# A transformer trunk whose feed-forward weights are summed on the fly: the third weight sum as a loaded block minus the first, on VectorE

## The chip, the cores and the metric

The kernel runs on one core of a Trainium2 chip. The metric is the device time of one execution in microseconds (us), lower is better. A core has TensorE (PE, matrix products; its weight loads are shown apart as PEld), VectorE (DVE), ScalarE (ACT), GpSimd (POOL) and SyncE (SP). Each of them works through its own list of instructions strictly in the order that was written. Loads from memory are issued by SP, ACT or POOL and carried out by 16 DMA engines that all share. In this kernel POOL issues only transfers that add what they carry to what stands at the target; plain loads are issued by SP.

## The reference

The reference is a small encoder trunk: 512 tokens and 16 learned meta tokens, width 1024, two layers. Each layer is

```python
h = h + 0.5 * swiglu(rmsnorm(h, gains[l, 0]), w_gate[l, 0], w_up[l, 0], w_down[l, 0])
h = h + mixer(rmsnorm(h, gains[l, 1]), ...)      # gated linear attention and softmax attention, merged
h = h + 0.5 * swiglu(rmsnorm(h, gains[l, 2]), w_gate[l, 1], w_up[l, 1], w_down[l, 1])
```

with `swiglu(x) = (silu(x @ w_gate) * (x @ w_up)) @ w_down`, gate and up 1024 x 2816, down 2816 x 1024, all in float32. A last norm follows, and the meta tokens are dropped. So there are four feed-forward parts (FFNs), named (layer, which) below: (0, 0), (0, 1), (1, 0), (1, 1). The change touches only them.

## The kernel before, in words

Every float32 matrix is split into a high and a low part in a rounded format that TensorE takes at a faster rate; a product is three matmuls (high x high, high x low, low x high). For each loaded or summed block of weights of 128 x 1024 values this means a copy on ScalarE that makes the high part (line 264) and a subtraction on VectorE that makes the low part (line 265). The pair is called the split.

The FFNs save matmuls with a scheme of seven block products where eight would be usual. The weights of an operation are four blocks, named 11, 12, 21 and 22, and the seven products, numbered 1 to 7, use these operands:

- products 1, 2 and 4: blocks 11, 12 and 22 as they are loaded (`DIRECT`);
- product 5: the first sum, 21 + 22 (`s1`);
- product 7: the third sum, 21 - 11 (`s3`);
- product 6: the second sum, 22 + 21 - 11 (`s2`);
- product 3: the fourth sum, 22 + 21 - 11 - 12 (`s4`).

An FFN has 15 such operations, numbered i. Numbers 0 to 10 are pairs of 128-column tiles of gate and up, in three groups of 4, 4 and 3 pairs. After each of the first two groups come two down quads (numbers 11 and 12, then 13 and 14), that is the part of the down product that belongs to the group; the third group's part is done in the usual way. Each product of an operation is 24 matmuls (lines 571 and 685). The order of all products is written out in `ffn_steps`: in a group, product 1 of the next pair comes ahead of product 7 of the current one, and so on, and in the change from a group to its quads the products of the last pair, the two quads and the next pair are interleaved.

The accumulators that TensorE fills are emptied by ScalarE (line 575, `snapshot`) and VectorE (lines 581 to 615). In the change to the quads VectorE and ScalarE also make the quads' operands from the pairs' results (lines 625, 646, 647, 651) and VectorE adds the quads' products to h (line 693).

`Weights` brings the blocks. `use(j)` first makes (splits) the loads up to a few ahead of product j and then fetches (issues the loads) up to nine ahead. Blocks go to a pool of three buffers (`raw`); `s3` and `s4` share three buffers (tag `wsa`, the long pool), `s1` and `s2` another three (tag `wsb`, the short pool). The sums are made so:

- `s3`: ScalarE writes the negated block 11 (`negative`, line 203), then POOL issues a transfer that adds block 21 from memory (`add`, line 208). This happens when block 11 is fetched (for the first two pairs of the first FFN, `OPENING`, when it is made).
- `s2`: SP loads block 22, then POOL issues a transfer that adds `s3` to it, from buffer to buffer.
- `s1`: SP loads block 21, then POOL issues a transfer that adds block 22 from memory.
- `s4`: for the first two pairs a negation of block 12 and a transfer that adds `s2`; from the third pair on VectorE subtracts block 12 from `s2` (line 233), when product 6 is made.

The order of each engine's instructions is not the order of the program. A planner simulates the kernel with its own estimates of durations and landings, and whenever an engine is free in that simulation it gives it the ready instruction that comes first in the program. So an instruction whose inputs the planner holds to be there may be placed ahead of others that stand earlier in the program and are not yet ready; on the chip the order is then fixed, and an engine waits at each instruction until its inputs have come. `W.behind` and `issue_after` keep the copies of line 264 behind certain instructions of ScalarE.

Of the kernel before, what the change touches and what calls it, by code (L numbers as in the profile page):

```python
# [14 lines left out]
ALU = mybir.AluOpType  # L15
# [31 lines left out]
OPENING = ((0, 0), 0), ((0, 0), 1)  # L47
# [101 lines left out]
NPAIR = FF // P // 2  # L149
# [21 lines left out]
class Weights:  # L171
# [34 lines left out]
    def add(self, t, src):  # L206

        self.nc.gpsimd.dma_start(t, src, accum_op=ALU.add)  # L208

    def sums(self, f, i, product, w):  # L210


        got = self.summed
        if product == "1":
            s3 = self.negative(f, i, "s3", w)
            self.add(s3, self.dram(f, i, "21"))
            s2 = self.block(f, i, "22", self.short, "wsb")
            self.add(s2, s3)
            got[f, i, "7"], got[f, i, "6"] = s3, s2
        if product == "12"[(f, i) in OPENING]:  # L220
            s1 = self.block(f, i, "21", self.short, "wsb")
            self.add(s1, self.dram(f, i, "22"))
            got[f, i, "5"] = s1
        late = 2 <= i
        if product == "2" and not late:
            s4 = self.negative(f, i, "s4", w)
            self.add(s4, got[f, i, "6"])
            got[f, i, "3"] = s4
        if product == "2" and late:
            self.kept = w  # L230
        if product == "6" and late:
            s4 = self.long.tile([P, SLAB], F32, tag="wsa", name=f"s4_{f[0]}{f[1]}_{i}")
            self.nc.vector.tensor_tensor(s4, w, self.kept, ALU.subtract)
            got[f, i, "3"] = s4

    def fetch(self, upto):

        while self.fetched < min(upto, len(self.loads)):
            load = self.loads[self.fetched]
            if isinstance(load, int):  # L240
                w = self.raw.tile([P, SLAB], F32, tag="raw", name=f"raw{load}")
                self.nc.sync.dma_start(w, self.wts[load])
                self.raws[self.fetched] = w
            elif load[2] in DIRECT:
                self.raws[self.fetched] = self.block(*load[:2], DIRECT[load[2]])
                if load[2] == "1" and load[:2] not in OPENING:
                    self.sums(*load, self.raws[self.fetched])
            self.fetched += 1

    def make(self, upto):  # L250
        nc = self.nc
        while self.made < min(upto, len(self.loads)):
            self.fetch(self.made + 1)
            s = self.made
            load = self.loads[s]
            w = self.raws.pop(s, None)
            if w is None:
                w = self.summed.pop(load)
            hi = self.hi_pool.tile([P, SLAB], F32R, tag="whi", name=f"whi{s}")
            lo = self.lo_pool.tile([P, SLAB], F32R, tag="wlo", name=f"wlo{s}")  # L260
            for a in np.split(np.arange(SLAB), 2 if s == 0 else 1):
                cs = slice(a[0], a[-1] + 1)
                with self.tc.issue_after(self.behind) if self.behind else nullcontext():
                    nc.scalar.copy(hi[:, cs], w[:, cs])  # L264
                nc.vector.tensor_tensor(lo[:, cs], w[:, cs], hi[:, cs].bitcast(F32), ALU.subtract)  # L265
            self.got[s] = (hi, lo)
            self.got.pop(s - 12, None)
            self.made += 1
            if not isinstance(load, int) and (load[2] in "26" or load[2] == "1" and load[:2] in OPENING):
                self.sums(*load, w)  # L270

    def use(self, j, ahead=AHEAD_MADE):
# [29 lines left out]
def build(tc, ctx, xt, wts, win, par, w2, const, umask, out):  # L302
# [243 lines left out]
    def ffn(l, f, norm, done, following):  # L546

        x, rs, up, n = norm.x, None, None, live[0]
        w = n // 2
        pools = open_pools("left", psum=("s2",), c=4, s2=2)  # L550
        made, hid, sums, raw, sets = {}, {}, {}, {}, {}
        risen = iter(range(KC))

# [636 lines left out]
    def finish_chunk(c):  # L1190
        fin.square(c)
        gain(c, slice(0, SEQ))

    def ending(sums, operand, rs):

        table("abs_reciprocal_sqrt_and_small")
# [146 lines left out]
```

## Time and profile before

| | before |
|---|---|
| median of 3 runs | 2238.69 us (2238.67 to 2239.18) |
| the profiled execution | 2233.24 us |
| its span, first to last instruction | 2231.4 us |
| granted TensorE clock, mean | 0.996 |
| TensorE busy | 2170.3 us, 97% |
| VectorE busy | 1700.7 us, 76% |
| ScalarE busy | 1244.2 us, 56% |
| POOL busy | 164.4 us, 7% |
| moved by DMA | 330.29 MB, 148 GB/s |

The page of the profile lists each engine's busy time, the costliest groups of instructions (line, engine, operation, output <- inputs, shape, count | busy us, mean ns of one | idle time ahead of them and what ended it), and the DMA issues with the median time from issue to landing. The list of waits says who waited for whom: us in total, times, longest. A row of the timeline is start, duration, engine, line, operation, and in brackets the idle time ahead of it and who ended it. A row of a table of stretches is the stretch, its length, then for TensorE, its weight loads, VectorE, ScalarE and POOL the busy us and the number of instructions, and last the granted clock, the share of the DMA engines and GB/s. In the names, `whi` and `wlo` are the high and low part of a block, `s` is a buffer of `s3` or `s4`, `w` any other block, `ss` an accumulator, `c` and `g` buffers of results and operands. The four FFNs lie at about 0 to 340, 750 to 1090, 1100 to 1450 and 1840 to 2200 us.

### The profile page before, as it was taken

What the parts mean: (1) busy time and instruction counts of PE and PEld (TensorE: products, weight loads), DVE (VectorE), ACT (ScalarE), POOL (GpSimd) and SP (SyncE); (2) the same over time, 40 slices, a digit from 0 to 9 for tenths busy, and PEclk for the clock granted to TensorE, in tenths of its full rate; (3) what the DMA queues carried; (4) which work ended last, traced back from release to release, by engine and by line L of the source; (5) the groups of instructions that cost most, each with busy time, mean ns of one, the idle gap of its engine ahead of it and who ended that gap; (6) DMA issues with size and microseconds to landing.
All of it is one profiled execution on the core that took longest, in us unless ns stands there. A gap on an engine that the chain in (4) does not pass through costs nothing. (4 is left out here: it accounts for less than half of the span.)

```text
span 2231.4 us, 40120 instructions
## 1 busy us (share of the span) xinstructions
PE 2170.3 (97%) x16506; PEld 2075.3 (93%) x16506; DVE 1700.7 (76%) x2623; ACT 1244.2 (56%) x1815; POOL 164.4 (7%) x192
## 2 busy tenths in 40 slices
PE   7999999999999999999999999999999999999898
PEld 7999999989999999999999999999788888999897
DVE  8877877577876679687788778676779768687777
ACT  8555555345784555454675455553557836545553
POOL 1111100000000011111011111000000001111100
PEclk9999999999999999999999999999999999999999
DMA  9877753212114577777668777421111237677761
GB/s 280 226 190 203 198 150 109 77 48 72 43 39 133 133 189 191 211 203 190 179 166 212 190 208 202 139 100 67 57 67 57 88 104 199 177 200 191 187 180 67
DMA packets 92647, 330.29 MB, mean 148 GB/s; under 512 B 10288, under 2 KB 12720, under 8 KB 92464
## 3 DMA queue, kind: packets, MB, share of 16 engines
q1 hardware_dynamic: 63440, 226.65, 28.2%
q0 software_dynamic: 27072, 98.58, 24.4%
q8 instruction: 130, 2.13, 0.4%
q10 hardware_dynamic: 1952, 2.50, 0.4%
q14 instruction: 53, 0.43, 0.1%
HBM read 289.94 MB, written 2.10 MB: 131 GB/s over the span
## 5 line engine op out<-in xcount | busy, mean ns | idle before, releaser
L571 PE MATMUL ss<-xc,whi 128*128 128x264 f32 (+1 forms) x4928 | 909.2, 286 | 26.1 <-ACT c L575 16.5
L571 PEld LDWEIGHTS ss<-xc,whi 128*128 128x128 f32 x4928 | 768.8, 190 | 31.1 <-ACT c L575 18.8
L571 PE MATMUL ss<-xc,wlo 128*128 128x264 f32 (+1 forms) x2464 | 702.8, 285 | 2.7 <-DVE wlo L265 2.7
L265 DVE TENSOR_TENSOR wlo<-w,whi 128x1024 fp32r<-128x1024 f32 (+1 forms) x301 | 365.3, 1216 | 152.8 <-ACT whi L264 152.7
L571 PEld LDWEIGHTS ss<-xc,wlo 128*128 128x128 f32 x2464 | 467.4, 190 | 4.3 <-DVE wlo L265 4.3
L264 ACT CAST whi<-w 128x1024 fp32r<-128x1024 f32 (+1 forms) x301 | 312.1, 1048 | 136.2 <-PE ss L571 52.2
L438 PE MATMUL mm<-x,whi 128*128 128x264 f32 (+1 forms) x1712 | 384.8, 315 | 0.0
L438 PEld LDWEIGHTS mm<-x,whi 128*128 128x128 f32 x1712 | 278.4, 188 | 16.6 <-issue 1.0
L438 PE MATMUL mm<-x,wlo 128*128 128x264 f32 (+1 forms) x856 | 266.1, 315 | 0.0
L685 PE MATMUL ss<-g,whi 128*128 128x264 f32 (+1 forms) x1280 | 239.5, 285 | 4.4 <-DVE h L693 3.1
L264 ACT CAST whi<-raw 128x1024 fp32r<-128x1024 f32 x126 | 132.0, 1048 | 163.6 <-PE mm L438 102.8
L685 PEld LDWEIGHTS ss<-g,whi 128*128 128x128 f32 x1280 | 198.6, 188 | 7.0 <-ACT whi L264 3.4
L265 DVE TENSOR_TENSOR wlo<-raw,whi 128x1024 fp32r<-128x1024 f32 x126 | 153.9, 1221 | 59.3 <-ACT whi L264 58.4
L685 PE MATMUL ss<-g,wlo 128*128 128x264 f32 (+1 forms) x640 | 181.2, 283 | 0.0
L575 ACT COPY c<-ss 128x528 f32<-128x528 f32 (+1 forms) x132 | 78.3, 593 | 181.6 <-PE ss L571 181.4
L265 DVE TENSOR_TENSOR wlo<-s,whi 128x1024 fp32r<-128x1024 f32 x120 | 146.5, 1221 | 37.5 <-ACT whi L264 37.5
L438 PEld LDWEIGHTS mm<-x,wlo 128*128 128x128 f32 x856 | 159.6, 188 | 8.5 <-issue 0.7
L438 PE MATMUL ss<-g,whi 128*128 128x264 f32 (+2 forms) x900 | 166.2, 299 | 0.0
L438 PEld LDWEIGHTS ss<-g,whi 128*128 128x128 f32 x900 | 131.7, 188 | 5.3
L264 ACT CAST whi<-s 128x1024 fp32r<-128x1024 f32 x120 | 126.1, 1051 | 10.9 <-PE ss L571 7.2
L208 POOL DMA_DIRECT2D w<-win x60 | 54.5, 908 | 1029.3 <-DVE wlo L265 410.3
L203 ACT ACTIVATE s<-w 128x1024 f32<-128x1024 f32 x68 | 71.6, 1056 | 89.7 <-DMA w<-win 77.9
(265 smaller groups left out, 3405.4 us busy)
## 6 DMA issues: line engine op xcount, KB each, us to landing
w<-win SPq DMA_DIRECT2D x299, 512.0 KB, 5.4
raw<-wts SPq DMA_DIRECT2D x126, 512.0 KB, 3.2
s<-win POOLq DMA_DIRECT2D x60, 512.0 KB, 5.2
w<-s POOLq DMA_DIRECT2D x60, 512.0 KB, 5.5
w<-win POOLq DMA_DIRECT2D x60, 512.0 KB, 7.5
s<-w POOLq DMA_DIRECT2D x8, 512.0 KB, 8.4
h<-xt SPq DMA_DIRECT2D x3, 528.0 KB, 6.3
out<-h ACTq DMA_DIRECT2D x4, 256.0 KB, 2.4
```

The lines of the kernel that those rows point to most:

```text
L203: self.nc.scalar.activation(t, w, AF.Copy, scale=-1.0)
L208: self.nc.gpsimd.dma_start(t, src, accum_op=ALU.add)
L264: nc.scalar.copy(hi[:, cs], w[:, cs])
L265: nc.vector.tensor_tensor(lo[:, cs], w[:, cs], hi[:, cs].bitcast(F32), ALU.subtract)
L438: TE.matmul(acc.half[i][:width], lhs, rhs[:, acc.spans[i]], start=first, stop=last)
L571: TE.matmul(acc[:, j], a[:, j, k], b[:, at], start=bool(begin and k == 0 and i == 0), stop=k == len(x) - 1 and i == 2, skip_group_check=no ...
L575: W.behind = S.copy(part(st, q), acc).ins
L685: TE.matmul(acc[:, j], a[:, j, k], xs[b][:, k], start=bool(begin and k == 0 and i == 0), stop=k == 3 and i == 2, skip_group_check=not begin)
```

## The change

For pairs from the third on and for all down quads (`2 <= i`) there is no negation any more. When block 11 is fetched, SP loads block 21 into the buffer of `s3` with a plain transfer, and block 22 into the buffer of `s2`. When product 1 has been made (block 11 has been split), VectorE subtracts block 11 from `s3` in place. The second sum then differs: for pairs (gate and up, `i < NPAIR`) VectorE adds `s3` to `s2` in place when product 2 has been made; for the quads POOL still issues the transfer that adds `s3` to `s2`, now after VectorE's subtraction. The first and the fourth sum are made as before, and the first two pairs of each FFN too.

```diff
+    def begin_sums(self, f, i, w=None):
         got = self.summed
-        if product == "1":
+        s3 = None
+        if i < 2:
             s3 = self.negative(f, i, "s3", w)
             self.add(s3, self.dram(f, i, "21"))
-            s2 = self.block(f, i, "22", self.short, "wsb")
+        else:
+            s3 = self.block(f, i, "21", self.long, "wsa")
+        s2 = self.block(f, i, "22", self.short, "wsb")
+        if i < 2:
             self.add(s2, s3)
+        got[f, i, "7"], got[f, i, "6"] = s3, s2
+        if (f, i) not in OPENING:
+            self.first_sum(f, i)
...
+        if (f, i) in OPENING and product in "12":
+            (self.begin_sums if product == "1" else self.first_sum)(f, i, *[w] * (product == "1"))
+        if i < 2:
+            if product == "2":
+                s4 = self.negative(f, i, "s4", w)
+                self.add(s4, got[f, i, "6"])
+                got[f, i, "3"] = s4
+        elif product == "1":
+            V.tensor_tensor(got[f, i, "7"], got[f, i, "7"], w, ALU.subtract)
+            if not i < NPAIR:
+                self.add(got[f, i, "6"], got[f, i, "7"])
+        elif product == "2":
             self.kept = w
-        if product == "6" and late:
+            if i < NPAIR:
+                V.tensor_tensor(got[f, i, "6"], got[f, i, "6"], got[f, i, "7"], ALU.add)
+        elif product == "6":
             s4 = self.long.tile([P, SLAB], F32, tag="wsa", name=f"s4_{f[0]}{f[1]}_{i}")
-            self.nc.vector.tensor_tensor(s4, w, self.kept, ALU.subtract)
+            V.tensor_tensor(s4, w, self.kept, ALU.subtract)
             got[f, i, "3"] = s4
...
                 if load[2] == "1" and load[:2] not in OPENING:
-                    self.sums(*load, self.raws[self.fetched])
+                    self.begin_sums(*load[:2], self.raws[self.fetched])
...
-            if not isinstance(load, int) and (load[2] in "26" or load[2] == "1" and load[:2] in OPENING):
+            if not isinstance(load, int) and load[2] in "126":
                 self.sums(*load, w)
```

`first_sum` holds the two lines that made `s1` before.

More of the change, by code (lines that the diff above doesn't have):

```diff
@@ L208, in add @@
         self.nc.gpsimd.dma_start(t, src, accum_op=ALU.add)
-    def sums(self, f, i, product, w):
+    def begin_sums(self, f, i, w=None):
         got = self.summed
-        if product == "1":
+        s3 = None
+        if i < 2:
             s3 = self.negative(f, i, "s3", w)
             self.add(s3, self.dram(f, i, "21"))
-            s2 = self.block(f, i, "22", self.short, "wsb")
+        else:
+            s3 = self.block(f, i, "21", self.long, "wsa")
+        s2 = self.block(f, i, "22", self.short, "wsb")
+        if i < 2:
@@ L218, in sums @@
             self.add(s2, s3)
[L219 to L229, printed above, removed]
+        got[f, i, "7"], got[f, i, "6"] = s3, s2
@@ new lines, in begin_sums, with first_sum, sums @@
+        if (f, i) not in OPENING:
+            self.first_sum(f, i)
+    def first_sum(self, f, i):
+        s1 = self.block(f, i, "21", self.short, "wsb")
+        self.add(s1, self.dram(f, i, "22"))
+        self.summed[f, i, "5"] = s1
+    def sums(self, f, i, product, w):
+        got, V = self.summed, self.nc.vector
+        if (f, i) in OPENING and product in "12":
[10 more added lines that the diff above has]
+        elif product == "2":
```

## The prediction

> **What bounds the kernel now.** I read the page's first part and its groups, then the waits, then the idle stretches of TensorE row by row, then what ScalarE and VectorE did ahead of the longest, and last the stretches in which VectorE is full. From the page, the list of waits and the groups by line:
>
> ```profile
> PE 2170.3 (97%) x16506; PEld 2075.3 (93%) x16506; DVE 1700.7 (76%) x2623; ACT 1244.2 (56%) x1815; POOL 164.4 (7%) x192
> L203 ACT ACTIVATE s<-w 128x1024 f32<-128x1024 f32 x68 | 71.6, 1056 | 89.7 <-DMA w<-win 77.9
> ACT s L203 <- DMA w<-win: 77.9, 18, 6.3
> PE ss L571 <- ACT c L575: 16.5, 11, 4.8
> L233 DVE TENSOR_TENSOR s<-w,w 128x1024 f32<-128x1024 f32 x52 | 63.4, 1219 | 0.1
> ```
>
> TensorE is busy for 97% of the span, so a change of helper work can win only what TensorE idles (2231.4 - 2170.3 = 61 us, its start and end among it) and what it loses to a lower clock. The second and third lines are the negations that the change removes: ScalarE stood 77.9 us at them, waiting for the block to land, 18 times and up to 6.3 us. Most of those stops cost nothing. The fourth line says where one may: TensorE waited 16.5 us for the copies at line 575 that empty its accumulators. These are its idle rows in the last FFN (first eight), and in an FFN before it at the same steps (last three):
>
> ```profile
> 1945.29 0.38 PE L571 MATMUL ss<-xc,whi 128*128 128x256 f32 x1 [4.84 <-ACT c L575]
> 1964.01 0.35 PE L685 MATMUL ss<-g,whi 128*128 128x256 f32 x1 [1.57 <-DVE h L693]
> 1964.72 0.38 PE L685 MATMUL ss<-c,whi 128*128 128x256 f32 x1 [0.24 <-ACT c L646]
> 1965.98 0.39 PE L685 MATMUL ss<-c,whi 128*128 128x256 f32 x1 [0.88 <-DVE c L647]
> 2076.43 0.58 PE L571 MATMUL ss<-xc,whi 128*128 128x256 f32 x1 [4.79 <-ACT c L575]
> 2095.91 0.35 PE L685 MATMUL ss<-g,whi 128*128 128x256 f32 x1 [1.51 <-DVE h L693]
> 2096.73 0.39 PE L685 MATMUL ss<-c,whi 128*128 128x256 f32 x1 [0.34 <-ACT c L646]
> 2097.99 0.39 PE L685 MATMUL ss<-c,whi 128*128 128x256 f32 x1 [0.88 <-DVE c L647]
> 854.58 0.39 PE L571 MATMUL ss<-xc,whi 128*128 128x264 f32 x1 [0.50 <-ACT c L575]
> 869.51 0.39 PE L685 MATMUL ss<-c,whi 128*128 128x264 f32 x1 [0.37 <-DVE c L647]
> 874.89 0.39 PE L685 MATMUL ss<-c,whi 128*128 128x264 f32 x1 [0.90 <-DVE c L647]
> ```
>
> Both long stops lie in the change from a group of pairs to its down quads. ScalarE in order of time shows why:
>
> ```profile
> 1935.81 0.83 ACT L646 CAST g<-g 128x768 fp32r<-128x768 f32 x1
> 1942.97 1.06 ACT L203 ACTIVATE s<-w 128x1024 f32<-128x1024 f32 x1 [6.33 <-DMA w<-win]
> 1943.93 0.81 ACT L646 CAST c<-g 128x768 fp32r<-128x768 f32 x1
> 1944.66 0.58 ACT L575 COPY c<-ss 128x512 f32<-128x512 f32 x1
> 2074.11 1.06 ACT L203 ACTIVATE s<-w 128x1024 f32<-128x1024 f32 x1 [6.27 <-DMA w<-win]
> ```
>
> The negation for the second quad, whose sum is due only ten products after the block itself, stood 6.33 us at the head of ScalarE; the cast of the operand and the copy that frees TensorE's accumulator were behind it. In the other three FFNs the planner put that copy ahead of the negation, and the same step costs 0.50 us. TensorE's clock fell after both stops:
>
> ```profile
> 1945.00:1950.00 5.00, 4.71 (x27) 4.72 (x28) 3.99 (x6) 2.25 (x4) 0.31 (x1) 0.66 0.58 107
> 1966.00:1970.00 4.00, 4.00 (x21) 4.00 (x22) 3.93 (x4) 0.00 (x0) 0.00 (x0) 0.57 0.02 4
> 2076.00:2083.00 7.00, 6.57 (x33) 6.58 (x34) 4.65 (x7) 3.48 (x5) 1.31 (x2) 0.55 0.52 95
> ```
>
> The number ahead of the last two is the granted clock. Time lost there is (1 - clock) x length.
>
> **The change, part by part.** Pairs 2 to 10 and the four quads are 13 third sums per FFN, 52 in all; 36 of them belong to pairs.
>
> Removed on ScalarE: 52 of the 68 negations, 52 x 1.056 = 54.9 us of an engine that is 56% busy. Their worth is the work that waited behind them.
> (1) The two long stops fall to the 0.50 of the other FFNs: (4.84 - 0.50) + (4.79 - 0.50) = 8.63 us.
> (2) What follows each: 1.57 + 0.24 + 0.88 = 2.69, and 1.51 + 0.34 + 0.88 = 2.73, against 0.37 + 0.90 = 1.27 elsewhere: 1.42 + 1.46 = 2.88 us.
> (3) The clock: 5 x 0.34 + 4 x 0.43 + 7 x 0.45 = 1.70 + 1.72 + 3.15 = 6.57 us.
> (4) Pair 2's negation also stood ahead of such a copy, waiting for a buffer, in two FFNs:
>
> ```profile
> 796.37 1.06 ACT L203 ACTIVATE s<-w 128x1024 f32<-128x1024 f32 x1 [2.52 <-DVE wlo L265]
> 797.96 0.39 PE L571 MATMUL ss<-xc,whi 128*128 128x264 f32 x1 [1.50 <-ACT c L575]
> 1884.18 0.39 PE L571 MATMUL ss<-xc,whi 128*128 128x256 f32 x1 [1.59 <-ACT c L575]
> ```
>
> (1.50 - 0.50) + (1.59 - 0.50) = 2.09 us. All other negations I cost at nothing gained: TensorE showed no idle row behind them.
>
> On (3) the Trainium skill has a rule: "TensorE: Matmul & The Clock Gate", the section on how the gate's oscillation bites, has the array fall to half rate once TensorE idled for a window of about 3.4 us. The first and third drop agree (4.84 and 4.79 us idle); the second does not, since the idle ahead of it was 1.57, 0.24 and 0.88 us. By that rule alone (3) would be 4.85 us and the forecast 1.7 us later.
>
> Added on VectorE: 36 x 2 + 16 = 88 additions and subtractions of 128x1024. Line 233 has the same form at 1219 ns, so 107.3 us of busy time (76% becomes 81%). In a row of full work one costs the pitch to the next, 1.14 us (856.99 to 858.13, below). Between group changes it is covered:
>
> ```profile
> 900.00:950.00 50.00, 50.00 (x412) 50.00 (x412) 33.12 (x39) 24.37 (x29) 6.65 (x8) 1.00 0.79 202
> 1150.00:1200.00 50.00, 49.27 (x404) 49.26 (x404) 42.76 (x58) 29.70 (x37) 6.09 (x7) 1.00 0.75 194
> 862.00:893.00 31.00, 29.65 (x235) 28.71 (x234) 30.52 (x37) 16.79 (x19) 3.49 (x4) 1.00 0.72 191
> ```
>
> At 412 matmuls in 50 us, a pair (7 products of 24) takes 20.4 us, in which VectorE (third number) is busy 33.12/50 x 20.4 = 13.5 us; 2 x 1.14 more leave 4.6 us idle. The second row is the fullest start of an FFN: 42.76 of 50, and some 2.5 pairs x 2.28 = 5.7 us more still fit. In the third, a group change, it is busy 30.52 of 31 us and has no cover. What I count there is two instructions ahead of the 0.90 us row: the second quad's subtraction, and the first quad's fourth sum, which today slips in early because its inputs are there, and which will wait for a later addition by POOL. Against that stands the idle time that today's negation makes on VectorE:
>
> ```profile
> 856.99 1.22 DVE L233 TENSOR_TENSOR s<-w,w 128x1024 f32<-128x1024 f32 x1
> 858.13 0.42 DVE L615 SCALAR_TENSOR_TENSOR c<-ss,rs 128x264 f32<-128x264 f32 x1
> 859.86 1.23 DVE L265 TENSOR_TENSOR wlo<-w,whi 128x1024 fp32r<-128x1024 f32 x1 [1.31 <-ACT whi L264]
> 861.36 0.43 DVE L625 TENSOR_TENSOR g<-c,ss 128x264 f32<-128x264 f32 x1 [0.27 <-ACT c L417]
> 857.83 1.06 ACT L203 ACTIVATE s<-w 128x1024 f32<-128x1024 f32 x1 [2.36 <-DMA w<-win]
> ```
>
> (5) 2 x 1.14 - (1.31 + 0.27) = 0.70 us per change, eight changes: 5.6 us lost. Bounds: nothing, if the planner finds other holes; 3 x 1.14 x 8 = 27.4 us if it finds none and the next pair's subtraction presses too. I take the value nearest to the rows of one change.
>
> Moved: block 21 comes by a plain transfer on SP in place of POOL's accumulating one (52), and 36 accumulating ones from buffer to buffer vanish.
>
> ```profile
> w<-win SPq DMA_DIRECT2D x299, 512.0 KB, 5.4
> s<-win POOLq DMA_DIRECT2D x60, 512.0 KB, 5.2
> w<-s POOLq DMA_DIRECT2D x60, 512.0 KB, 5.5
> SPq L198 <- DVE wlo L265: 666.0, 145, 15.7
> ```
>
> SP gets 52 issues more, each behind a buffer of the long pool that until now the negation waited for. Later in that queue stand the second and the third plain block of the pair; but SP stands up to 15.7 us at such frees already, for the load of block 21 that follows, and every load is issued eight loads ahead of its use, so I cost the issue at 0, and at the most at what a late buffer cost TensorE before, the 2.09 us of (4). POOL loses 88 issues, and what queues behind them (the sum 21 + 22) comes earlier: 0, since no row shows a cast waiting for it. The new wait on VectorE is for block 21's landing: it lands one transfer after block 11, and the subtraction's turn is behind block 11's own split, about six products after the issue: 0, and at the most the second rival's price. If the planner pulls it early into a hole, everything on VectorE queues behind it; that is the second rival.
>
> Sum: -8.63 - 2.88 - 6.57 - 2.09 + 5.6 = -14.6 us. The profiled execution took 2233.24 us, so 2218.6; the median of the runs, 2238.69, stands 5.45 above that execution, and with the same offset the forecast is 2224 us.
>
> **The rivals.** *VectorE becomes the bound in the group changes.* For it speaks the row 862 to 893; against it the holes that vanish with the negations. The gains of 20.2 us are used up at 20.2 / 8 = 2.5 us per change, that is 2.2 uncovered instructions. At the upper bound: 2238.69 - 20.2 + 27.4 = 2245.9. The Trainium skill ("Perfetto Trace Analysis", on the most-contended engine) would judge such a stretch by VectorE's occupancy, 98% there, and so put all added work on the path; the trace before disagrees in part, since TensorE still had 29.65 of 31 us.
>
> *The same trap on VectorE: slower.* The planner believes block 21 landed, pulls a subtraction into a hole, and VectorE stands there as ScalarE did. One such stop is worth half of (1) to (3), 18.08 / 2 = 9.0 us. For it: that is how the negations stood 18 times. Against it: line 233, which is also pulled early, waited 0.1 us in 52 times. Three in place of today's two give 2224.1 + 27.1 = 2251; it decides from two on.
>
> *The stop stays.* The planner writes a new order, and some other instruction (a split whose block is late) takes the place ahead of the copies; only (4) and (5) are seen: 2238.69 - 2.09 + 5.6 = 2242. For it: the plain blocks still take 5.4 us to land; against it: a split's turn is some six products later than the negation's.
>
> **How the numbers follow.** The forecast gets 0.64, faster in all its range. VectorE as the bound gets 0.16, about evenly a small gain, no difference and a loss (0.05, 0.05, 0.06); the trap 0.12, slower; the stop that stays 0.08, no difference that a measurement of this kernel can tell (0.2%, 4.5 us). So faster 0.69, same 0.13, slower 0.18. The likeliest one's own range is 2213 (nothing lost in (5), and 5 us of the shorter waits for line 575 gone too, of their 16.5) to 2233 (little over a third of the gain). The whole range goes up to the first rival's end, 2246, and leaves out the trap with three stops.
>
> **What would show it.** After: no row at line 203 beyond the first two pairs; no idle row of 4 us at line 571 in the last FFN, and a granted clock of 1.00 there; ScalarE near 1189 us, VectorE near 1808; the 0.90 us rows of the group changes grown to some 1.6. It is wrong if VectorE shows stops of several us for a landing, or if the 862 to 893 stretch shows TensorE idle for 3 us more than now.

## The result and the profile after

The changed kernel took 2265.93 us (median; 2258.84 to 2267.80) beside 2238.93 for the kernel before on the same chip: ratio 1.0112, 95% interval 1.0088 to 1.0135. It is slower by 1.1%, 25 us, where 2224 us was forecast, and it lies above the range. Below, a ratio is turned into us by (ratio - 1) x 2239.

The profiled execution took 2266.88 us, span 2265.0. Line 243 is the new subtraction, 249 the new addition; other lines have moved (571 to 590, 575 to 594, 591 to 610, 264 and 265 to 283 and 284, 685 to 704, 693 to 712, 233 to 252). From the page of after, its first part and the groups:

```profile
PE 2187.3 (97%) x16506; PEld 2088.2 (92%) x16506; DVE 1798.7 (79%) x2711; ACT 1195.4 (53%) x1763; POOL 87.6 (4%) x104
...
L243 DVE TENSOR_TENSOR w<-w,w 128x1024 f32<-128x1024 f32 x52 | 63.6, 1222 | 59.6 <-DMA w<-win 53.2 <-issue 6.4
```

From its list of waits (us in total, times, longest):

```profile
DVE w L243 <- DMA w<-win: 53.2, 24, 6.3
...
PE ss L590 <- DVE wlo L284: 14.4, 16, 4.5
...
PE ss L590 <- DVE c L610: 8.1, 7, 1.9
...
PE ss L704 <- DVE h L712: 8.1, 7, 1.5
...
PE ss L590 <- ACT c L594: 6.3, 11, 0.7
```

The stops that the change was to remove are gone: line 594, which answers to line 575 before, cost TensorE 16.5 us with a longest of 4.8, and costs 6.3 with a longest of 0.7. In their place VectorE stands at its new subtraction, 24 times and up to 6.3 us, waiting for block 21 to land. Before, it stood nowhere for such a landing. The rows of VectorE that show it, at the start of the first FFN (first two), in a group change (the next four) and in the last FFN's first group change (last):

```profile
50.05 1.23 DVE L243 TENSOR_TENSOR w<-w,w 128x1024 f32<-128x1024 f32 x1 [2.96 <-DMA w<-win]
...
66.55 1.22 DVE L243 TENSOR_TENSOR w<-w,w 128x1024 f32<-128x1024 f32 x1 [6.34 <-DMA w<-win]
...
877.81 1.23 DVE L243 TENSOR_TENSOR w<-w,w 128x1024 f32<-128x1024 f32 x1 [2.66 <-DMA w<-win]
878.96 0.98 DVE L666 TENSOR_TENSOR c<-g,c 128x792 fp32r<-128x792 f32 x1
879.85 0.70 DVE L610 TENSOR_TENSOR c<-c,ss 128x528 f32<-128x528 f32 x1
...
886.99 1.22 DVE L284 TENSOR_TENSOR wlo<-w,whi 128x1024 fp32r<-128x1024 f32 x1
...
1979.60 1.22 DVE L243 TENSOR_TENSOR w<-w,w 128x1024 f32<-128x1024 f32 x1 [3.52 <-DMA w<-win]
```

By the order of the loads, the row at 886.99 is the split of the block that the subtraction at 877.81 uses: the subtraction runs 9 us ahead of it.

And TensorE at those places, and in the last FFN at the first of the two old stops:

```profile
53.08 0.39 PE L590 MATMUL ss<-xc,wlo 128*128 128x264 f32 x1 [2.68 <-DVE wlo L284]
69.65 0.59 PE L590 MATMUL ss<-xc,wlo 128*128 128x264 f32 x1 [4.46 <-DVE wlo L284]
...
880.70 0.48 PE L590 MATMUL ss<-xc,whi 128*128 128x264 f32 x2 [0.91 <-DVE c L610]
881.74 0.39 PE L590 MATMUL ss<-xc,wlo 128*128 128x264 f32 x1 [0.56 <-DVE wlo L284]
...
1977.48 0.50 PE L590 MATMUL ss<-xc,whi 128*128 128x256 f32 x2 [0.70 <-ACT c L594]
1982.44 0.47 PE L590 MATMUL ss<-xc,whi 128*128 128x256 f32 x2 [1.86 <-DVE c L610]
1983.48 0.39 PE L590 MATMUL ss<-xc,wlo 128*128 128x256 f32 x1 [0.57 <-DVE wlo L284]
```

Behind the stop at 877.81 waits the sum at line 610 that empties an accumulator; TensorE idles 0.91 us for it, and 0.56 for the split behind that. At 1977.48 the old stop of 4.84 us is now 0.70, but 5 us later, behind the stop of 3.52 us at 1979.60, TensorE idles 1.86 + 0.57 us for VectorE. Last, stretches of the clock (the number ahead of the last two):

```profile
69.00:76.00 7.00, 6.35 (x30) 6.35 (x31) 7.00 (x9) 1.04 (x1) 0.00 (x0) 0.52 0.00 0
...
894.90:898.30 3.40, 1.17 (x6) 0.57 (x4) 3.40 (x5) 3.40 (x4) 0.00 (x0) 1.00 0.61 176
898.30:901.70 3.40, 3.38 (x15) 3.38 (x16) 3.40 (x4) 0.53 (x2) 0.00 (x0) 0.51 0.02 5
...
1975.00:1990.00 15.00, 11.87 (x84) 11.28 (x83) 11.30 (x15) 6.35 (x8) 0.87 (x1) 0.89 0.62 174
```

The two profiled executions differ by 2265.0 - 2231.4 = 33.6 us of span. TensorE's idle time grew by (2265.0 - 2187.3) - (2231.4 - 2170.3) = 16.6 us, and the same 16506 matmuls took 2187.3 - 2170.3 = 17.0 us more, at a mean granted clock of 0.990 against 0.996, which by itself gives 2170.3 x (0.996 / 0.990 - 1) = 13 us. So about half the loss is idle time, and most of the other half a slower clock. The profiled execution of before is 5.45 us faster than its median, so this gap is wider than the 25 us.

### The profile page after: what moved, and what is told of

The parts are those of the page before. It is cut to its first block, busy times and chain, and to the rows that moved or that the text cites. A ratio compares the mean times of both kernels' runs of the same rounds, so it can differ in the third digit from the quotient of the medians.

```text
span 2265.0 us, 40086 instructions
## 1 busy us (share of the span) xinstructions
PE 2187.3 (97%) x16506; PEld 2088.2 (92%) x16506; DVE 1798.7 (79%) x2711; ACT 1195.4 (53%) x1763; POOL 87.6 (4%) x104
## 5 line engine op out<-in xcount | busy, mean ns | idle before, releaser
L590 PE MATMUL ss<-xc,whi 128*128 128x264 f32 (+1 forms) x4928 | 913.6, 287 | 24.7 <-ACT whi L283 8.4
L284 DVE TENSOR_TENSOR wlo<-w,whi 128x1024 fp32r<-128x1024 f32 (+1 forms) x353 | 427.0, 1217 | 76.6 <-ACT whi L283 76.2
L283 ACT CAST whi<-w 128x1024 fp32r<-128x1024 f32 (+1 forms) x353 | 366.4, 1048 | 180.1 <-PE ss L590 77.2
L457 PEld LDWEIGHTS mm<-x,whi 128*128 128x128 f32 x1712 | 279.2, 189 | 16.5 <-issue 1.0
L436 ACT ACTIVATE c<-c 128x528 f32<-128x528 f32 (+1 forms) x88 | 56.5, 642 | 132.5 <-DVE c L634 132.2
L704 PEld LDWEIGHTS ss<-g,wlo 128*128 128x128 f32 x640 | 121.9, 190 | 2.5 <-DVE wlo L284 2.5
L704 PE MATMUL ss<-c,whi 128*128 128x264 f32 (+1 forms) x512 | 104.1, 296 | 7.1 <-ACT c L665 5.3
```

What stands on the lines that cost most here:

```text
L436: prev_act[0] = S.activation(*args, **kw).ins
L457: TE.matmul(acc.half[i][:width], lhs, rhs[:, acc.spans[i]], start=first, stop=last)
L590: TE.matmul(acc[:, j], a[:, j, k], b[:, at], start=bool(begin and k == 0 and i == 0), stop=k == len(x) - 1 and i == 2, skip_group_check=no ...
L704: TE.matmul(acc[:, j], a[:, j, k], xs[b][:, k], start=bool(begin and k == 0 and i == 0), stop=k == 3 and i == 2, skip_group_check=not begin)
```

## The experiments

The theory after the result: the planner puts the new subtractions ahead of their landing, and the stops cause the loss. The rival: the added VectorE work itself costs that much, wherever it stands. They are told apart by moving the work without removing it, and by adding the work without the change.

**Place: all new work behind the splits.** Each subtraction and addition may be issued only behind the low part of the split of the block that it uses.

```diff
-                nc.vector.tensor_tensor(lo[:, cs], w[:, cs], hi[:, cs].bitcast(F32), ALU.subtract)
+                self.split_end = nc.vector.tensor_tensor(lo[:, cs], ..., ALU.subtract).ins
...
-            V.tensor_tensor(got[f, i, "7"], got[f, i, "7"], w, ALU.subtract)
+            with self.tc.issue_after(self.split_end):
+                V.tensor_tensor(got[f, i, "7"], got[f, i, "7"], w, ALU.subtract)
```

> The changed kernel, with each new subtraction and addition of VectorE put behind the split of the block after which it stands in the program, so that the planner can't pull it ahead into a hole; the work is the same. If the loss is VectorE standing at subtractions whose block hasn't landed (theory of the stop), the waits of 53.2 us at line 243 vanish, and with them the two long stops at the start of the first FFN (9.9 us) and the 3 us stops in the eight group changes: about 2224 us, as the sum of the prediction had it. If the loss is the 88 added instructions on a full VectorE (theory of the work), the order doesn't help: 2255 us or more.

2240.31 us, ratio 1.0002 [0.9992, 1.0011]: no different from before, and 25 us better than the change as it was. From the waits of this kernel:

```profile
PE ss L706 <- ACT c L667: 11.6, 8, 2.4
DVE s L254 <- DMA w<-w: 10.2, 8, 2.5
```

No wait for a landing is left at the subtraction. A smaller stop takes its place: the quads' fourth sum (line 254) now reads a second sum that POOL's transfer is still adding to. The place of the instructions, not their number, makes the difference between the changed kernel and this one; but the expected gain is still missing.

**Place: one group at a time.** Only the quads' subtractions behind their splits, and only the pairs' subtractions and additions.

```diff
+            with self.tc.issue_after(self.split_end) if not i < NPAIR else nullcontext():   # only the quads
...
+            with self.tc.issue_after(self.split_end) if i < NPAIR else nullcontext():       # only the pairs
```

> As the first, but only the subtractions of the down quads are put behind the split; those of the pairs may still be pulled ahead. Theory of the stop: the group changes are freed, the start of the first FFN keeps its 9.9 us: 2234 us. Theory of the work: 2255 us or more. If the pairs' stops elsewhere cost much too, it stays above 2245.

> The changed kernel with only the pairs' subtractions and additions behind their splits; the quads' subtractions stay where the planner puts them. With all behind it took 2240.3, with only the quads' 2246.5, as it is 2265.9. If the stops add up: 2265.9 - (2246.5 - 2240.3) = 2259.7, and it shows the eight stops of 2.4 to 3.5 us at the second quad's subtraction but not the two at the first FFN's start. If the pairs' early places cause the quads' stops, near 2246.

Only the quads: 2246.53 us, ratio 1.0031 [1.0018, 1.0043]. Only the pairs: 2257.07 us, 1.0073 [1.0058, 1.0089]. The waits at the subtraction, first of the kernel with the quads behind, then of the one with the pairs behind:

```profile
DVE w L244 <- DMA w<-win: 29.0, 14, 6.8
```

```profile
DVE w L244 <- DMA w<-win: 24.7, 8, 4.0
...
PE ss L592 <- DVE c L612: 8.8, 6, 2.2
```

The stops of the change are of two kinds: those of the pairs (14 in the first kernel, 16 of the 24 in the changed one), worth 6.9 - 0.4 = 6.5 us, and eight of the quads, worth 16.3 - 0.4 = 15.9 us. With the 0.4 us of all behind, that is 22.8 of 25.1 us, well inside the intervals. The quads' stops are shorter (24.7 us in all) but cost more than twice as much: they lie in the group changes.

**Work alone, a first try.** The kernel before, with an instruction on `s3` and `s2` where the change has one (a maximum of a buffer with itself, which leaves the values as they are).

```diff
+            if not isinstance(load, int) and load[1] >= 2 and (load[2] == "1" or load[2] == "2" and load[1] < NPAIR):
+                t = self.summed[load[0], load[1], "7" if load[2] == "1" else "6"]
+                with self.tc.issue_after(self.split_end):
+                    nc.vector.tensor_tensor(t, t, t, ALU.max)
```

> The kernel before, with negations and accumulating transfers as they were, and 88 instructions of 128x1024 more on VectorE, each the maximum of a third or second sum with itself, which changes nothing, behind the same splits as in the first run and on data that has long landed. Theory of the work: most of the loss, 2255 to 2266 us. Theory of the stop: the sum's own term for the added work, 5.6 us without the holes that the negations made (1.58 us per group change), so 5.6 to 18 us: 2244 to 2257, and the stops of 4.8 us in the last FFN stay.

2322.17 us, ratio 1.0376 [1.0351, 1.0402]. This misses as a price of work, as its waits show:

```profile
DVE s L274 <- DMA w<-s: 105.7, 29, 11.1
```

The maximum had to wait for POOL's transfer that still read `s3`. It tells something else: 105.7 us of stops on VectorE, with the work, cost 84 us of the kernel's time.

**Work alone, clean.** The same 88 instructions on the blocks 11 and 12 themselves, which have landed and been split by then; then the 16 of the quads and the 72 of the pairs each alone.

```diff
+            if not isinstance(load, int) and load[1] >= 2 and (load[2] == "1" or load[2] == "2" and load[1] < NPAIR):
+                with self.tc.issue_after(self.split_end):
+                    nc.vector.tensor_tensor(w, w, w, ALU.max)
...
+            if not isinstance(load, int) and NPAIR <= load[1] and load[2] == "1":          # the 16 of the quads
...
+            if not isinstance(load, int) and 2 <= load[1] < NPAIR and load[2] in "12":     # the 72 of the pairs
```

> The kernel before with 88 instructions of 128x1024 more on VectorE, at the places where the first run has its subtractions and additions, each the maximum of block 11 or 12 with itself, written in place. Their input has landed and no transfer reads it afterwards, which was not so in the earlier run of this kind. It prices the added work on its own: by the prediction's bounds 5.6 to 27.4 us over before, that is 2245 to 2267; by the theory of the stop at the lower end, by the theory of the work at the upper.

> The kernel before with 16 of the 88 added instructions only: each quad's block 11 takes the maximum of itself with itself, behind its own split (the output stays the reference's). The 88 together cost 22.8 us (2262.8 against 2240.0). If VectorE's work costs where it is full, in the eight group changes, to which these 16 belong, each costs about its pitch of 1.14 us: 2240 + 16 x 1.14 = 2258, and the pairs' 72 almost nothing. If every instruction costs alike: 2240 + 22.8 x 16 / 88 = 2244.

> The kernel before with the other 72: blocks 11 and 12 of pairs 2 to 10 take the maximum of themselves with themselves behind their splits. If VectorE's work costs only in the group changes: at most 2240 + (22.8 - 18.2) = 2245, from the two pairs that follow each change. If every instruction costs alike: 2240 + 22.8 x 72 / 88 = 2259.

All 88: 2262.82 us, ratio 1.0105 [1.0090, 1.0120], 23.5 us. The 16: 2261.41 us, 1.0096 [1.0081, 1.0111], 21.5 us. The 72: 2244.22 us, 1.0017 [1.0007, 1.0026], 3.8 us. So 18% of the instructions make nearly all of the cost: 21.5 / 16 = 1.34 us each in the group changes (1.13 to 1.55 by the interval, so their pitch of 1.14 or more), and 3.8 / 72 = 0.05 us elsewhere. TensorE in the group change that the prediction looked at, with the 16, in the stretch in which it idled 0.37 and 0.90 us before:

```profile
877.17 0.64 PE L688 MATMUL ss<-g,whi 128*128 128x264 f32 x3 [1.23 <-ACT g L649]
878.54 0.39 PE L688 MATMUL ss<-g,whi 128*128 128x264 f32 x1 [0.25 <-DVE g L650]
...
884.27 0.48 PE L688 MATMUL ss<-g,whi 128*128 128x264 f32 x2 [1.12 <-DVE h L696]
885.67 0.39 PE L688 MATMUL ss<-c,whi 128*128 128x264 f32 x1 [0.92 <-ACT c L649]
```

and the clock there:

```profile
884.00:892.00 8.00, 6.81 (x40) 6.56 (x41) 7.31 (x9) 3.99 (x5) 0.00 (x0) 0.79 0.14 57
```

Four short idle rows, 3.52 us together, and then 8 x 0.21 = 1.7 us lost to the clock. From the page of the same kernel:

```profile
PE 2182.6 (97%) x16506; PEld 2087.4 (92%) x16506; DVE 1717.0 (76%) x2639; ACT 1243.9 (55%) x1815; POOL 164.4 (7%) x192
```

Against the profile of before the span is 28.5 us longer, of which the same matmuls took 12.3 us more; the rest, 16.2, is idle time. VectorE waits for no transfer in this kernel, so there is no stop of the other kind in it. The idle time lies at the quads' products: TensorE's waits at their matmuls (line 688; 685 before) are 27.8 us in all against 13.8 before, which is 14.0 of the 16.2. The largest of before, then of this kernel:

```profile
PE ss L685 <- DVE c L647: 9.4, 14, 0.9
```

```profile
PE ss L688 <- ACT c L649: 12.9, 8, 2.4
PE ss L688 <- ACT g L649: 7.8, 6, 1.6
```

**The gain alone.** The kernel before, with the quads' negation and its two accumulating transfers moved behind the copy of the load just ahead of product 1; then the same with the quads' fourth sum behind the split of product 6.

```diff
+        elif product == "1":                                   # quads, when block 11 is fetched
+            got[f, i, "6"] = self.block(f, i, "22", self.short, "wsb")
+            self.held.append((self.at[f, i, "1"] - 1, f, i, w))
...
+            while self.held and self.held[0][0] <= s:          # in make, behind the split of load s
+                _, f, i, b = self.held.pop(0)
+                with self.tc.issue_after(copied):
+                    s3 = self.negative(f, i, "s3", b)
+                self.add(s3, self.dram(f, i, "21"))
+                self.add(self.summed[f, i, "6"], s3)
+                self.summed[f, i, "7"] = s3
...
+            with self.tc.issue_after(self.split_end) if i >= NPAIR else nullcontext():     # the second kernel alone
                 self.nc.vector.tensor_tensor(s4, w, self.kept, ALU.subtract)
```

> The kernel before, in which only the quads' negations (16 of 68) and the two accumulating transfers behind each come later: behind the ScalarE copy of the load just ahead of the quad's product 1. If terms (1) to (3) of the prediction are right, the two stops of 4.8 us in the last FFN and the lower clock behind them go: 2238.9 - 18.1 = 2221 us. If the planner's new order only moves the stop, 2236 us or more.

> The kernel before with the quads' negations later, as in the fourth run, and the quads' fourth sum put behind the split of product 6. In the fourth run that sum waited 43.4 us for the second sum's transfer, 8 times and up to 5.8 us, and the gain of 18 us never showed. Theory of the stop: without those waits the loss of the fourth run goes and the gain comes: 2221 to 2230 us. If the gain isn't there to be had, 2238 or more.

The first: 2251.42 us, ratio 1.0050 [1.0035, 1.0065], slower by 0.5%. Its waits name the reason, the trap again, one instruction further: VectorE at the fourth sum, whose input now lands later.

```profile
DVE s L238 <- DMA w<-s: 43.4, 8, 5.8
...
PE ss L697 <- DVE g L637: 15.2, 8, 2.6
```

The second: 2226.63 us, 0.9939 [0.9922, 0.9956]: 13.7 us faster, the interval from 9.9 to 17.5. Where the first old stop of the last FFN stood, TensorE's timeline from 1930 to 1962 us has one idle row:

```profile
1948.76 0.50 PE L584 MATMUL ss<-xc,whi 128*128 128x256 f32 x2 [0.43 <-ACT c L588]
```

Most of the gain that the prediction saw is there, and can be had by order alone.

**The change in the quads, without its stops.** All behind the splits and the quads' fourth sum too; the same with the quads' second sum on VectorE instead of POOL; and the change in the quads only, while the pairs keep the negation.

```diff
+            with self.tc.issue_after(self.split_end) if i >= NPAIR else nullcontext():     # all three
                 V.tensor_tensor(s4, w, self.kept, ALU.subtract)
...
-            if i < NPAIR:                                                                  # the second
+            if i < NPAIR + 4:
                 V.tensor_tensor(got[f, i, "6"], got[f, i, "6"], got[f, i, "7"], ALU.add)
...
-        if i < 2:                                                                          # the third, in begin_sums
+        if i < NPAIR:
             s3 = self.negative(f, i, "s3", w)
```

> The first run again, in which also the quads' fourth sum (VectorE, 16 instructions) is put behind the split of product 6, so that it can't be pulled ahead of the transfer that completes the second sum. In the first run it waited 10.2 us for that transfer, 8 times and up to 2.5 us, in the midst of the group changes. Theory of the stop: those waits vanish, and with them some 1.3 to 2 us in each group change: 2224 to 2230 us. Theory of the work (the group changes are full, whatever the order): 2240 us as in the first run.

> As the run with the fourth sum put behind, but the quads' second sum is an addition on VectorE too (16 instructions more, behind the split of product 2) and no transfer of POOL is left behind a subtraction. No instruction of VectorE waits for a transfer that was issued late. Theory of the stop: no slower than the run before it by more than 16 x 1.14 / 2 = 9 us, and faster where the transfer was still late. Theory of the work: 8 x 2.28 = 18 us slower than that run.

> The change in the quads alone (block 21 by a plain transfer, the subtraction behind its block's own split, the fourth sum behind the split of product 6); the pairs keep ScalarE's negation as before. The gain of the late negation in the quads was 13.4 us (2226.6 against 2240.0). If the 16 subtractions cost 1.14 us each, nothing is left: 2240 - 13.4 + 18 = 2245. If they cost 0.26 us each: 2240 - 13.4 + 4 = 2231, and then it is the pairs' 72 instructions that use the gain up.

In this order: 2238.43 us, ratio 0.9997 [0.9987, 1.0006]; 2242.83 us, 1.0013 [1.0004, 1.0022]; and 2241.74 us, 1.0011 [1.0002, 1.0020]. In the first of them VectorE waits for no transfer any more, and yet it is no faster than with the waits of 10.2 us: the fourth sum's place is worth no more than the intervals here. Sixteen more instructions in place of POOL's transfers cost 3.6 us, 0.22 each, much less than the 1.34 above: what an instruction costs in a group change depends on where in it it stands, and I did not find out by what rule. The third closes the account of the quads: 13.7 us won by the stops that go, 2.5 us lost on balance, so what the change puts in their place, the 16 subtractions above all, costs 16.2 us, 2.0 us per change (give or take 4 us in all, by the two intervals). The trace of the third shows the same wait as the kernel with the 16 alone:

```profile
PE ss L704 <- ACT c L665: 12.8, 8, 2.0
```

TensorE waits eight times for the cast of the operand c. That row stands at 10.3 to 13.1 us in every kernel that has 16 or 32 instructions more on VectorE at the quads, behind the splits and on landed blocks, and at 7.3 us at most in those that have none. In the profiled execution of the third, TensorE's idle time is 2244.4 - 2183.3 = 61.1 us, as before; the whole 13.0 us of longer span are longer matmuls, at a clock of 0.989 against 0.996.

**The pairs.** The quads with the late negation (2226.63), and the pairs as changed, behind their splits; and the kernel before with every negation from the third pair on late, without and with the pairs' fourth sum behind the split of product 6.

```diff
+        elif i < NPAIR:                                        # the first: pairs as changed
             s3 = self.block(f, i, "21", self.long, "wsa")
+        else:                                                  # quads: late negation
+            self.held.append((self.at[f, i, "1"] - 1, f, i, w))
...
-        if product == "1" and i < NPAIR:                       # the second and third
+        if product == "1" and i < 2:
...
-            with self.tc.issue_after(self.split_end) if i >= NPAIR else nullcontext():     # the third
+            with self.tc.issue_after(self.split_end):
                 self.nc.vector.tensor_tensor(s4, w, self.kept, ALU.subtract)
```

> The change in the pairs alone, each subtraction and addition behind its block's split, and in the quads ScalarE's late negation with the fourth sum behind (2226.6 with the old pairs). The pairs' 72 instructions cost 4.7 us when added alone (2244.2 against 2239.5). If that price holds in full and the removed negations and transfers of the pairs are worth nothing: 2231. If they are worth what the sums so far leave for the pairs (all changed and pinned, 2238.4, less the quads alone, 2241.7: 3.3 us better): 2223.

> As the late negation of the quads with their fourth sum behind, 2226.6, but with the negations and two accumulating transfers of pairs 2 to 10 moved behind the copy of the load ahead of product 1 as well. If the only harm of an early negation in the pairs is the stop of pair 2 ahead of the copy in two FFNs, 2.09 us by the prediction: 2224.5. If the later transfers make the sums 21 - 11 and 21 + 22 - 11 late for their casts: above 2230, with TensorE idle for a split of a sum in every pair.

> As all negations later (2286.1), with the fourth sum of the pairs too behind the split of product 6. There VectorE stood 172.0 us at that sum, 28 times and up to 10.3, waiting for the accumulating transfer. If that early place is the cause, the 46 us go: near 2227, and at most 4.5 us off. If the later transfers themselves are late for their casts: still above 2240, with ScalarE standing at the split of product 6.

The first: 2224.96 us, ratio 0.9931 [0.9916, 0.9945], 15.4 us faster than before and the best of all; from the old pairs' 13.7 it differs by less than the intervals, so the pairs' half of the change costs nothing and wins nothing that can be measured. From its page, and the last FFN's first group change in its table of stretches:

```profile
PE 2171.9 (98%) x16506; PEld 2076.3 (93%) x16506; DVE 1784.3 (80%) x2695; ACT 1211.4 (54%) x1779; POOL 102.1 (5%) x120
```

```profile
1930.00:1962.00 32.00, 31.44 (x264) 31.02 (x262) 28.42 (x39) 20.51 (x26) 5.32 (x6) 1.00 0.73 182
```

VectorE is as busy as in the slow kernel (80% against 79%), TensorE is busy 31.44 of 32 us, at full clock. The end of the same change is less clean, as TensorE's idle rows and the stretches there show:

```profile
1964.35 0.47 PE L715 MATMUL ss<-g,whi 128*128 128x256 f32 x2 [1.01 <-ACT g L676]
1965.30 0.38 PE L715 MATMUL ss<-c,whi 128*128 128x256 f32 x1 [0.48 <-ACT c L676]
1965.99 0.39 PE L715 MATMUL ss<-g,wlo 128*128 128x256 f32 x1 [0.31 <-DVE wlo L288]
```

```profile
1962.00:1966.00 4.00, 2.20 (x16) 1.62 (x14) 4.00 (x6) 2.74 (x3) 0.00 (x0) 1.00 1.00 172
1966.00:1970.00 4.00, 4.00 (x23) 4.00 (x24) 4.00 (x5) 1.25 (x2) 0.00 (x0) 0.64 1.01 316
```

The second: 2286.13 us, 1.0205 [1.0183, 1.0227], far off; the third: 2236.45 us, 0.9984 [0.9974, 0.9993]. The waits of the second, and of the third:

```profile
DVE s L239 <- DMA w<-s: 172.0, 28, 10.3
...
PE ss L584 <- DVE wlo L271: 43.7, 27, 8.6
```

```profile
ACT whi L270 <- DMA w<-s: 33.4, 16, 5.3
...
PE ss L584 <- DVE wlo L271: 5.8, 9, 1.0
```

Moving the pairs' fourth sums wins back 45.9 + 3.6 = 49.5 us. The rest of the distance to 2226, 10 us, I put down to the later transfers, for which ScalarE stands 33.4 us at splits; that was not tried apart.

## Why the prediction was wrong

**(1), the two long stops:** right in itself. The row at 1977.48 has 0.70 us where 4.84 were, 4.1 of the 4.3 forecast for that stop.

**(2) and (3), what follows the stops, and the clock:** right in part as a mechanism, not for this kernel. With the stops removed by order alone, (1) to (3) gave 13.7 us of the 18.1. In the best version the clock of 0.66 right behind the first stop is 1.00. The idle rows that follow went only from 2.69 to 1.01 + 0.48 + 0.31 = 1.80 us, not to the 1.27 forecast, and the clock behind them, 0.57 before, is 0.64 and not 1.00. In the changed kernel both were given back some us later: 1.86 + 0.57 us idle for VectorE where 2.69 stood, and a clock of 0.89 over 15 us, 1.65 us lost, against 3.42 in the two stretches of before.

**(4), pair 2's negation:** it is gone (line 203 is left with the first two pairs' 16 instructions), but no run measured its 2.09 us apart; the pairs' half as a whole showed no difference.

Two steps failed: the price of the added work (5), and the wait on VectorE for block 21, which the sum has at 0. The second is the larger.

**(5), the added work, is the first step that failed.** "I take the value nearest to the rows of one change", 0.70 us per change, 5.6 in all. Measured alone it is 23.5 us, near the upper bound of 27.4, and in the changed quads, where the idle time behind the negation is won back, 16.2 us by the difference of two runs, 2.0 per change. Two things were wrong. The holes of 1.31 and 0.27 us that I counted as room, 12.6 us over eight changes, gave back about 21.5 - 16.2 = 5.3, a difference of three runs that is hardly clear of their intervals. And I counted VectorE's time only: in the group change shown, the delay comes out as several idle rows of TensorE of about 1 us, and then the clock falls. What I said of the work between group changes nearly held: 72 instructions, put at 0, for 3.8 us. This is the first rival's mechanism, at 0.16. The sentence from the Trainium skill ("Perfetto Trace Analysis", the section on the most-contended engine) judges a stretch by the occupancy of VectorE. For the 98% stretch it was nearer than my reading of TensorE's 29.65 of 31 us: 16 x 1.14 = 18.2 us, measured 21.5.

**The wait on VectorE for block 21's landing, put at 0, is the second step that failed.** The sum gives as the reason that "the subtraction's turn is behind block 11's own split, about six products after the issue". Nothing in the changed kernel holds it there: the subtraction reads blocks 11 and 21 as they are loaded, and nothing that the split makes. In the trace it ran 9 us ahead of that split, at 877.81 against 886.99, and waited 2.66 us; there are 24 such stops, 53.2 us, and they cost 6.5 + 15.9 = 22.4 us of the kernel's time. With the place that the sum assumed, behind the splits, the wait is gone.

This is the second rival, the trap on VectorE, at 0.12. It was described rightly, with its place (a subtraction pulled into a hole before block 21 landed) and its trace. It was priced wrongly: not two or three stops of 9 us but eight in the group changes at 15.9 / 8 = 2.0 us, and the pairs' stops, 6.5 us. And I thought it unlikely for a reason that did not bear: line 233 "waited 0.1 us in 52 times" while its inputs came early. The same fourth sum stood 172.0 us when its input came later. Its row tells of its inputs, not of the planner's care.

Together: -13.7 for the stops that go, +16.2 for the quads' work, about nothing for the pairs, +22.4 for the stops that come, 24.9 against 25.1 measured. Each of these terms is known to 4 us or so, so that they add up this closely is luck.

## What to carry to other kernels

Where an order is planned ahead, an instruction that waits for a transfer on an in-order engine is a stop for all that queues behind it: tie it behind something that must come later anyway, and then look which instruction is the next to be late, since three moves here only shifted the stop to the next instruction, the fourth sum. Price added work by the stretch that it falls into: where a helper engine is full and TensorE already shows idle rows, count its full time, and expect a lower clock on top, and count holes as room only where something is seen to fill them. Look whether a gain can be had by order alone, without new work: here 13.7 us could.

## What the runs showed of the hardware

The clock falls without one long pause. In after, from 894.90 to 898.30 us, TensorE was busy 1.17 of 3.40 us, in pieces, its longest idle row 1.47 us, and the 3.40 us that follow ran at 0.51. With the quads' work alone, 3.52 us of idle time in four rows, none over 1.23 us, led to 0.79 over 8 us. In the best version 1.80 us in three rows led to 0.64 over 4 us, but the same three rows 124 us later (1.01, 0.48 and 0.31 us, up to 2090.45) left the clock at 1.00: the sum of the idle time alone does not decide it, and what does is open. The Trainium skill ("TensorE: Matmul & The Clock Gate", the section on how the gate's oscillation bites) warns of idle gaps above about 3.4 us; here a stretch of that length with a third of the work in it was enough, and the measurement decides.

The plain transfers from `win`, among them the 52 that the change made plain, landed in 4.4 us (median of 351) against 5.4 before (299). That was still too late for where the subtraction stood.
